# Output projection with prepared weight rows, and a down projection in parts of 3, 4 and 4: one edit to a decoder trunk on one core

## The chip, the cores and the metric

The kernel runs on one core of a Trainium2 chip. The metric is the device time of one launch in microseconds (us); of several executions the median counts. A profile shows one execution, and its span runs from the first to the last instruction. The engines are TensorE (PE in the profile; its weight loads are PEld), VectorE (DVE), ScalarE (ACT), GpSimd (POOL) and SyncE (SP), which here issues nearly all DMAs in one queue. Each engine runs its own instructions in program order.

## The reference, cut to what matters

One decoder layer on 2048 tokens (T) of width 1024 (D), all in float32. Two mixers share one input projection. Each one's output is normalised by its own RMS and gain, the two are put side by side and go through one output projection with a residual; then comes a SwiGLU block of hidden width 2816, and a last norm.

```python
def rmsnorm(x, g):
    return x * rsqrt(mean(x * x, axis=-1) + 1e-6) * g

h = rmsnorm(x, norm_mix)
u_a, z_b, xbc_b, dt_b = split(h @ w_in)
y_a = rmsnorm(s5_mixer(u_a, ...), s5_norm)        # 1024 columns
y_b = rmsnorm(ssd_mixer(z_b, xbc_b, dt_b, ...), ssd_norm)   # 1024 columns
x = x + concatenate([y_a, y_b], axis=-1) @ w_out  # w_out: 2048 x 1024
h = rmsnorm(x, norm_ffn)
x = x + (silu(h @ w_gate) * (h @ w_up)) @ w_down  # w_down: 2816 x 1024
return rmsnorm(x, norm_final)
```

The factor `rsqrt(...)` belongs to a token (a "norm factor" below), the gain `g` to a channel (a "channel factor").

## The kernel before, in words

**Products.** A float32 product is made of three matmuls: each operand is split into a high and a low part, and high x high, high x low and low x high add up in one PSUM bank. A split is a copy on ScalarE (high) and a subtraction on VectorE (low; in the input projections on GpSimd, L69).

**Stages, in order of time.** First the input projections of token half 0 (`project` with tiles `us`, `xs`, `zs`: S5 inputs, convolution channels, gate), beside which VectorE makes the S5 tables (`s5_tables`, about 123 to 241 us); the same for half 1; then the S5 scans, the SSD mixer in quarters and the gated linear unit of S5 (`glu`) to 1213 us. From there on all products are of the Winograd form (L1130): a 2 x 2 block product in seven block products instead of eight, of sums of blocks. One call of `winograd` has seven products `P1` to `P7`; each takes n row blocks x three matmuls of 128 x 512 (L1155), so 84 matmuls with n = 4 and 63 with n = 3. The stationary operands (A11, A12, A22 and the sums S1 to S4) come from tokens, the moving ones (B11 to B22 and the sums T1 to T4) from weights or, in the up part, the other way round. The seven results are added to residual tiles `x`: an "end" is one addition on VectorE out of PSUM (L1161); a "kept" partial sum, on which a later product goes on in the same bank, is copied by ScalarE into a small tile `sg` (L1166), and VectorE adds the copy (L1168).

**Output projection** (`mixed_out`, 1213 to 1585 us). Round r = 0 takes the S5 rows of w_out, r = 1 the SSD rows, each with eight tiles of 256 tokens. For a tile, `normed` (L1194) loads the tokens `st`, makes a diagonal matrix `dg` of their norm factors (L1202), spreads it over all partitions by a matmul with ones (`ps_iv`, L1204), and multiplies each of eight channel blocks by channel factor and norm factor (L1208). `stationary_operands` (L1100) then makes and splits the seven operands of the tile, VectorE doing the sums and low parts (L976). Seven splits of B operands happen once for each round: those of r = 0 ahead of its first tile in `mixed_out`, those of r = 1 within the last tile of r = 0 by `next_rows` (L1067), which loads raw weight blocks, makes the sums T1 to T4 on VectorE between the splits, and hangs each split behind the product that frees its buffer (`after`, L1169). During the last tiles of r = 1, `NextTokens` (L1030) prepares the first operands of the up part and transposes tokens on TensorE (L151). After each tile of r = 1 the norm factors of its two 128-token chunks come out of `norm_stats` (L87): about eight small instructions on VectorE for each chunk.

**Up part** (`ffn_up`): two token halves of 22 calls each, 1585 to 2467 us.

**Down projection** (`ffn_down`, L1328): three rounds over the rows of w_down, each adding to the residual that a DRAM array carries (`x1D`, `x2D`, `x3D`; load at L1350, store at L1356). The rounds have n = 4, 4 and 3 (`down_rows`, L1317), eight tiles of 256 tokens each. The turn from one round to the next is made by `next_rows` again. In the last round a tile also gets its final norm: squares on ScalarE (L1363), the factor on VectorE (`norm_stats`), the multiplication by factor and gain (L1367), and the store of the output (L1368). The `x` tiles come from one tag of four buffers (`t4`), two for each tile of tokens.

**What sets the order.** The program is written stage by stage, but a list scheduler with a simulated time line places the instructions on each engine; `high_priority()` moves a block ahead, and `issue_after(i)` keeps it behind instruction i. A tile waits for its buffer until the last reader of the one before has finished. `take(i, ...)` gives the large slot s*i*.

## Time and profile before

| what | value |
|---|---|
| median of 3 runs | 2949.43 us (2948.5 to 2951.28) |
| the profiled execution | 2948.97 us, its span 2947.2 us |
| mean granted TensorE clock | 0.976 of full speed |
| PE, PEld busy | 95%, 76% of the span |
| DVE, ACT, POOL busy | 71%, 40%, 19% |
| HBM read, written | 263.86 MB, 132.12 MB |

How to read the rows that follow. A group of instructions has line, engine, operation, output <- inputs (names without buffer numbers), partitions x elements and count; then busy us, mean ns of one; then the idle time just ahead of them and what ended most of it. A stretch (`from:to`) has its length and the busy time of PE, PEld, DVE, ACT and POOL (with counts), the granted clock, the mean busy share of the DMA engines, and GB/s; a short form has only PE and PEld. A wait has engine and operation, what it waited for, the sum in us, the count and the longest.

### The profile page before, as it was taken

What the parts mean: (1) busy time and instruction counts of PE and PEld (TensorE: products, weight loads), DVE (VectorE), ACT (ScalarE), POOL (GpSimd) and SP (SyncE); (2) the same over time, 40 slices, a digit from 0 to 9 for tenths busy, and PEclk for the clock granted to TensorE, in tenths of its full rate; (3) what the DMA queues carried; (4) which work ended last, traced back from release to release, by engine and by line L of the source; (5) the groups of instructions that cost most, each with busy time, mean ns of one, the idle gap of its engine ahead of it and who ended that gap; (6) DMA issues with size and microseconds to landing.
All of it is one profiled execution on the core that took longest, in us unless ns stands there. A gap on an engine that the chain in (4) does not pass through costs nothing.

```text
span 2947.2 us, 35852 instructions
## 1 busy us (share of the span) xinstructions
PE 2797.5 (95%) x13020; PEld 2244.4 (76%) x13020; DVE 2087.4 (71%) x3937; ACT 1177.6 (40%) x1853; POOL 550.2 (19%) x462
## 2 busy tenths in 40 slices
PE   7999999998999989899898999998999999999986
PEld 6777877777877867687676888886888887878875
DVE  7398049989768788988789555557555558686786
ACT  4244234556553343433335333334333334243442
POOL 2364111124666767200000000000000000000000
PEclk9999999999999999899999999999999999999998
DMA  7256345543446464644553222223322224555444
GB/s 182 80 158 195 107 133 153 165 131 100 135 145 193 148 185 128 197 168 147 143 169 118 86 86 86 96 80 100 112 86 81 73 78 173 175 179 193 164 142 136
DMA packets 314873, 398.33 MB, mean 135 GB/s; under 512 B 32492, under 2 KB 232280, under 8 KB 314696
## 3 DMA queue, kind: packets, MB, share of 16 engines
q1 hardware_dynamic: 314696, 396.04, 42.6%
q8 instruction: 103, 1.69, 0.2%
q14 instruction: 74, 0.61, 0.1%
HBM read 263.86 MB, written 132.12 MB: 134 GB/s over the span
## 4 chain that ended last, share of the span: by engine, by line
PE 41%; DVE 10%; DMA 6%; issue 1%; ACT 0%; SPq 0%; DVEq 0%; ACTq 0%
PE ps_w L1155 40%; DMA s<-ybD 2%; DVE s L976 2%; DMA out_dram<-x 1%; DVE x L1161 1%; DVE s L1208 1%; DMA s<-actD 1%; DVE s L1014 1%; DVE wS L976 1%; DVE wA L976 1%; DMA x<-x3D 1%; DVE x L1168 1%; DVE x L1367 0%; DMA x<-xaD 0%; DVE sum L1115 0%
## 5 line engine op out<-in xcount | busy, mean ns | idle before, releaser
L1155 PE MATMUL ps_w<-s,wS 128*128 128x512 f32 x3936 | 956.8, 397 | 32.6 <-DVE s L976 14.0
L1155 PEld LDWEIGHTS ps_w<-s,wS 128*128 128x128 f32 x3936 | 746.9, 190 | 207.2 <-DVE s L976 16.1
L1155 PE MATMUL ps_w<-s,wA 128*128 128x512 f32 x2952 | 738.3, 402 | 33.2 <-DVE x L1161 11.9
L1155 PEld LDWEIGHTS ps_w<-s,wA 128*128 128x128 f32 x2952 | 564.6, 192 | 172.1 <-DVE x L1161 11.8
L971 ACT CAST wS<-sum 128x512 fp32r<-128x512 f32 (+1 forms) x336 | 203.6, 611 | 394.5 <-PE ps_w L1155 201.6
L81 PE MATMUL ps_in<-s,whi 128*128 128x512 f32 x896 | 352.9, 395 | 0.0
L83 PE MATMUL ps_in<-s,wlo 128*128 128x512 f32 x896 | 351.4, 394 | 1.3 <-POOL wlo L69 1.3
L82 PE MATMUL ps_in<-s,whi 128*128 128x512 f32 x896 | 352.2, 393 | 0.0
L976 DVE TENSOR_TENSOR wS<-sum,wS 128x512 fp32r<-128x512 f32 (+1 forms) x336 | 226.2, 676 | 137.7 <-ACT wS L971 137.1
L69 POOL TENSOR_TENSOR wlo<-wst,whi 128x1024 fp32r<-128x1024 f32 x72 | 183.9, 2555 | 371.2 <-ACT whi L66 344.8
L971 ACT CAST wA<-s 128x512 fp32r<-128x512 f32 (+1 forms) x252 | 150.4, 610 | 249.1 <-PE ps_w L1155 166.4
L1161 DVE TENSOR_TENSOR gu<-ps_w,gu 128x512 f32<-128x512 f32 x134 | 92.5, 691 | 153.6 <-PE ps_w L1155 150.0
L83 PEld LDWEIGHTS ps_in<-s,wlo 128*128 128x128 f32 x896 | 168.9, 189 | 40.1 <-issue 3.4
L81 PEld LDWEIGHTS ps_in<-s,whi 128*128 128x128 f32 x896 | 168.8, 188 | 38.7 <-issue 3.1
L82 PEld LDWEIGHTS ps_in<-s,whi 128*128 128x128 f32 x896 | 168.9, 188 | 36.5 <-issue 2.3
L832 POOL TENSOR_TENSOR s<-cm,dtas 128x512 fp32r<-128x512 f32 x128 | 165.9, 1321 | 44.3 <-PE ps_seg L833 44.3
L976 DVE TENSOR_TENSOR wA<-s,wA 128x512 fp32r<-128x512 f32 (+1 forms) x252 | 165.2, 673 | 3.4 <-ACT wA L971 3.3
L1161 DVE TENSOR_TENSOR x<-ps_w,x 128x512 f32<-128x512 f32 x160 | 109.1, 688 | 52.4 <-PE ps_w L1155 52.1
L1166 ACT COPY gu<-ps_w 128x512 f32<-128x512 f32 x134 | 78.1, 585 | 142.7 <-PE ps_w L1155 141.0
L1168 DVE TENSOR_TENSOR x<-x,sg 128x512 f32<-128x512 f32 x125 | 85.5, 688 | 66.4 <-ACT sg L1166 37.6
L760 DVE SCALAR_TENSOR_TENSOR acc<-xp,cols,acc 128x1024 f32<-128x1024 f32 x72 | 109.4, 1519 | 26.6 <-ACT acc L758 26.0
L66 ACT CAST whi<-wst 128x1024 fp32r<-128x1024 f32 x72 | 75.4, 1047 | 119.6 <-PE ps_in L82 73.2
(356 smaller groups left out, 3614.5 us busy)
## 6 DMA issues: line engine op xcount, KB each, us to landing
wst<-in_w_in_dram SPq DMA_DIRECT2D x56, 512.0 KB
s<-in_w_gate_dram SPq DMA_DIRECT2D x22, 1024.0 KB
s<-in_w_up_dram SPq DMA_DIRECT2D x22, 1024.0 KB
actD<-gu SPq DMA_DIRECT2D x44, 512.0 KB
s<-actD SPq DMA_DIRECT2D x16, 1024.0 KB
xD<-xo SPq DMA_DIRECT2D x24, 512.0 KB
uD<-ev SPq DMA_DIRECT2D x16, 512.0 KB
zD<-sz SPq DMA_DIRECT2D x32, 256.0 KB
```

The source lines that it names most:

```text
L69: eng.tensor_sub(lo, st, hi.bitcast(F32))
L81: nc.tensor.matmul(ps, wh[:, i, :], rh[:, i, :], start=(i == 0), stop=False)
L82: nc.tensor.matmul(ps, wh[:, i, :], rl[:, i, :], start=False, stop=False)
L83: last = nc.tensor.matmul(ps, wl[:, i, :], rh[:, i, :], start=False, stop=(i == n - 1))
L760: V.scalar_tensor_tensor(acc, tap(i), col(i), acc, op0=MUL, op1=ADD)
L832: G.tensor_mul(r, bc(k.tri.unsqueeze(1), [P, 4, P]), bc(part, [P, 4, P]))
L971: a = k.nc.scalar.copy(op[:, 0], raw)
L976: b = eng.tensor_sub(op[:, 1, part], raw[:, part], op[:, 0, part].bitcast(F32))
L1155: nc.tensor.matmul(ps, a[:, p, i, :], b[:, q, i, :], start=(root == name and i == 0 and p + q == 0), stop=(i == n - 1 and p == 1), skip_gr ...
L1161: V.tensor_add(dst, ps, dst if onto else src)
L1166: nc.scalar.copy(dst, bank[root])
L1168: V.tensor_add(block, block, dst)
```

## The change

Four edits go together.

1. **w_out is prepared early, on GpSimd.** A new function `out_rows` runs 16 times between the pairs of tiles of `xs` and `zs` in half 0: two steps follow each pair. A step loads a row block of w_out (of four row blocks, half the columns), multiplies it by the channel factors (2 instructions), makes the sums T1 to T4 (4 subtractions) and stores all eight blocks to a new DRAM array `woD`. In return the low parts of these input weights (L69) are made on VectorE (`lo_pool=False`).
2. **The output projection reads the prepared blocks and leaves the tokens as they are.** `made_rows` takes the place of `next_rows` for r = 1 and only loads and splits. `tokens` takes the place of `normed`: the load alone, without `dg`, `ps_iv` and L1208. Instead `winograd` gets a `scale`: since a row of a product belongs to a token, the norm factor is applied to ends (one VectorE instruction that multiplies and adds) and to kept results (in the ScalarE copy).
3. **Norm factors elsewhere.** In r = 1 `norm_stats` runs once per tile for two chunks, on GpSimd in tiles 0 to 6, on VectorE in the last. The last four additions of squares in `glu` go from GpSimd to VectorE.
4. **Down projection.** The rounds get n = 3, 4, 4 (`PARTS`). In the last round one of a tile's two `x` tiles comes from three further buffers in a free slot, and the final norm's factors are made for both chunks at once, on GpSimd in tiles 0 to 6.

Its core as a diff:

```diff
@@ norm_stats
-    V = k.nc.vector
+    V = k.nc.gpsimd if pool else k.nc.vector
...
-        V.scalar_tensor_tensor(i, t, 1.5, y, op0=ADD, op1=MUL)
+        if pool:
+            V.tensor_scalar(t, t, 1.5, None, ADD)
+            V.tensor_mul(i, t, y)
+        else:
+            V.scalar_tensor_tensor(i, t, 1.5, y, op0=ADD, op1=MUL)
@@ project_pairs
-            w = split_w(k, k.w_in[:, c0 : c0 + P], lo_pool=True)
+            w = split_w(k, k.w_in[:, c0 : c0 + P], lo_pool=lo_pool)
@@ glu
-                nc.gpsimd.tensor_add(sums[:, b], sums[:, b], sq)
+                (V if half and i == KD - 2 else nc.gpsimd).tensor_add(sums[:, b], sums[:, b], sq)
@@ winograd
+    row = {"P2": 0, "P3": 0, "P7": 1, "P4": 1}
+    row_kept = {"P1": 0, "P6": 0, "P5": 1, "P7": 1}
...
-            V.tensor_add(dst, ps, dst if onto else src)
+            if scale:
+                V.scalar_tensor_tensor(dst, ps, scale[row[name]], dst, op0=MUL, op1=ADD)
+            else:
+                V.tensor_add(dst, ps, dst if onto else src)
...
-            nc.scalar.copy(dst, bank[root])
+            if scale:
+                nc.scalar.activation(dst, bank[root], AF.Identity, scale=scale[row_kept[name]])
+            else:
+                nc.scalar.copy(dst, bank[root])
...
+OPS = ("B11", "B12", "B21", "B22", "T1", "T2", "T3", "T4")
+def out_rows(k, w_out, q, area):
+    nc, G = k.nc, k.nc.gpsimd
+    r, kk, e = q // 8, q // 2 % 4, q % 2
+    t = area[:, q % 2]
+    for i in range(2):
+        b = t[:, 2 * i : 2 * i + 2]
+        row = r * 8 + i * 4 + kk
+        src = w_out[row * P : row * P + P, :].rearrange("p (a n) -> p a n", a=2)
+        nc.sync.dma_start(b, src[:, :, e * 256 : e * 256 + 256])
+        G.tensor_scalar(b, b, k.cols[:, C_S5N + row : C_S5N + row + 1], None, MUL)
+    b11, b12, b21, b22, t1, t2, t3, t4 = (t[:, i] for i in range(8))
+    G.tensor_sub(t1, b12, b11)
+    G.tensor_sub(t2, b22, t1)
+    G.tensor_sub(t3, b22, b12)
+    G.tensor_sub(t4, b21, t2)
+    nc.sync.dma_start(k.woD[r, kk, :, :, e * 256 : e * 256 + 256], t)
+def made_rows(k, old, load):
+    m = Moving(k, 4)
+    x = k.spare
+    t = k.take(x, [P, 2, 4, 512], F32)
+    load(t[:, 0], "B11")
+    load(t[:, 1], "T1")
+    r = {}
+    def p1():
+        m.split("B11", old.at["B11"], t[:, 0])
+        load(t[:, 0], "T3")
+    def p2():
+        k.spare = old.at["B21"]
+        r["y"] = k.take(k.spare, [P, 2, 4, 512], F32)
+        load(r["y"][:, 0], "T2")
+        load(r["y"][:, 1], "B22")
+    def p6():
+        m.split("T1", old.at["T2"], t[:, 1])
+        load(t[:, 1], "B21")
+    def p5():
+        m.split("T2", old.at["T1"], r["y"][:, 0])
+        load(r["y"][:, 0], "T4")
+    def p4():
+        m.split("B21", old.at["T4"], t[:, 1])
+        m.split("T4", x, r["y"][:, 0])
+    return m, {
+        "P1": p1,
+        "P2": p2,
+        "P6": p6,
+        "P5": p5,
+        "P7": lambda: m.split("B22", old.at["T3"], r["y"][:, 1]),
+        "P3": lambda: m.split("T3", old.at["B22"], t[:, 0]),
+        "P4": p4,
+    }
@@ mixed_out
+        return lambda dst, name: nc.sync.dma_start(dst, k.woD[r, :, :, OPS.index(name)].rearrange("k p n -> p k n"))
...
-    def normed(r, c, behind=None):
+    def tokens(r, c):
...
-        dg = sp.tile([P, 2, P], F32, name="dg", tag="sq", bufs=1)
-        inv = k.yinv if r else k.ainv
-        for i in range(2):
-            V.tensor_scalar(dg[:, i], k.ident, inv[:, 2 * c + i : 2 * c + i + 1], None, MUL)
-        ps = (k.px)([P, 256], "ps_iv")
-        nc.tensor.matmul(ps, k.ones, dg.rearrange("p a b -> p (a b)"), start=True, stop=True)
-        col = C_SSDN if r else C_S5N
-        with k.tc.issue_after(behind) if behind else nullcontext():
-            for kk in range(KD):
-                V.scalar_tensor_tensor(st[:, kk], st[:, kk], k.cols[:, col + kk : col + kk + 1], ps, op0=MUL, op1=MUL)
...
+        load(x[:, 0], "B11")
+        load(x[:, 1], "T1")
+        st = tokens(0, 0)
+        load(y[:, 0], "T2")
+        load(y[:, 1], "B22")
+        B.split("B11", 7, x[:, 0])
+        B.split("T1", 8, x[:, 1])
...
+        load(x[:, 0], "T3")
+        load(x[:, 1], "B21")
+        B.split("T2", s[1], y[:, 0])
+        load(y[:, 0], "T4")
+        B.split("B22", s[2], y[:, 1])
+        B.split("T3", s[4], x[:, 0])
+        B.split("B21", s[3], x[:, 1])
+        t4 = B.split("T4", s[0], y[:, 0])
...
-                    nextB, ops = next_rows(k, B, 4, load_of(1))
+                    nextB, ops = made_rows(k, B, load_of(1))
...
-                norm_stats(k, k.ss, k.inv, slice(ch, ch + 1))
+            if r:
+                norm_stats(k, k.ss, k.inv, slice(2 * c, 2 * c + 2), pool=c < 7)
+PARTS = ((3, 0), (4, 6), (4, 14))
@@ down_rows
-        n = (4, 4, 3)[r]
+        n, first = PARTS[r]
@@ ffn_down
-                gf = k.take(k.spare, [P, D], F32)
+                area = k.take(k.spare, [P, 4, D], F32)
+                gf = area[:, 0]
...
-                x.append(sp.tile([P, 2, 512], F32, name="x2", tag="t4", bufs=4))
+                if r == 2 and i:
+                    x.append(area[:, 1 + c % 3].rearrange("p (a n) -> p a n", a=2))
+                else:
+                    x.append(sp.tile([P, 2, 512], F32, name="x2", tag="t4", bufs=4))
...
+            for q in (slice(0, 1), slice(1, 2)) if late else (slice(0, 2),):
+                (V if late else nc.gpsimd).tensor_add(s[:, 0, q], s[:, 0, q], s[:, 1, q])
+                norm_stats(k, s[:, 0], iv, q, pool=not late)
@@ trunk_kernel
+    k.woD = dp.tile([2, 4, P, 8, 512], F32, name="woD")
...
-        project(k, 0, h, xs)
+        todo = list(range(16))
+        area = k.take(3, [P, 2, 8, 256], F32)
+        for _ in project_pairs(k, 0, h, xs, lo_pool=False):
+            for _ in range(2):
+                out_rows(k, ins["w_out"][0], todo.pop(0), area)
...
-            project(k, 0, h, zs)
+            for _ in project_pairs(k, 0, h, zs, lo_pool=False):
+                for q in todo[:2]:
+                    out_rows(k, ins["w_out"][0], q, area)
+                todo = todo[2:]
```

**Where instructions move.** VectorE, second round of the output projection, before; `dg`, `nt` and `inv` belong to the norm factors, `s_10406` is the token buffer, `x_` a residual tile, `wS_` an operand:

```order
L1202 TENSOR_SCALAR dg<-cm,yinv 128x128
L1168 TENSOR_TENSOR x_12090<-x_12090,sg 128x512
L976 TENSOR_TENSOR wS_12232<-sum,wS_12232 128x512
L104 SCALAR_TENSOR_TENSOR inv<-nt,ng 128x1
L100 SCALAR_TENSOR_TENSOR nt<-ng,nv 128x1
L104 SCALAR_TENSOR_TENSOR inv<-nt,inv 128x1
L1208 SCALAR_TENSOR_TENSOR s_10406<-s_10406,cols,ps_iv 128x256 x8
```

The same place on VectorE in the changed kernel (`s_10552` is the token buffer):

```order
L1168 SCALAR_TENSOR_TENSOR x_12060<-ps_w,yinv,x_12060 128x512
L980 TENSOR_TENSOR wA_12190<-s_10552,wA_12190 128x512
L1168 SCALAR_TENSOR_TENSOR x_11907<-ps_w,yinv,x_11907 128x512
L980 TENSOR_TENSOR wS_12050<-sum,wS_12050 128x512
L1168 SCALAR_TENSOR_TENSOR x_11905<-ps_w,yinv,x_11905 128x512
```

The steps for the factors and the multiplication of the tokens are gone from VectorE's queue; the additions carry the factor (`yinv`).

GpSimd, while VectorE makes the S5 tables, before; `BD` belongs to the tables, `xp` and `tail` are the convolution's input and its last columns:

```order
L69 TENSOR_TENSOR wlo<-wst,whi 128x1024
L751 COPY xp<-xp 128x8x3x15
L752 COPY xp<-xp 128x7x3
L754 COPY tail<-xp 128x3
L494 MEMSET BD 128x256
```

The same stretch on GpSimd now (`s_1682` is the row block of w_out):

```order
L757 COPY xp<-tail 128x3
L1201 TENSOR_SCALAR s_1682<-s_1682,cols 128x512
L755 COPY xp<-xp 128x8x3x15
L756 COPY xp<-xp 128x7x3
L758 COPY tail<-xp 128x3
L1203 TENSOR_TENSOR s_1682<-s_1682 128x256
```

The low parts have left the queue, and the scalings and subtractions of the row blocks stand between the convolution's copies.

SyncE in the same stretch, before; `wst` are the next input weights, `m1D`, `qD` and `m2D` the stored S5 tables:

```order
L483 DMA m1D<-M_1258 128x1024
L492 DMA qD<-W 128x8x128
L64 DMA wst<-in_w_in_dram 128x8x128
L512 DMA m2D<-Ks 8x16x128
L512 DMA m2D<-Ks 8x16x112
```

And now:

```order
L487 DMA m1D<-M_1259 128x1024
L496 DMA qD<-W 128x8x128
L1207 DMA woD<-s_1682 1024x1x256 x2
L64 DMA wst<-in_w_in_dram 128x8x128
L516 DMA m2D<-Ks 8x16x128
```

Two stores of finished row blocks (`woD`) stand ahead of the load of the next input weights.

## The prediction

> **What bounds the kernel now.** I read first the page's line of busy times. Then I cut the fused Winograd matmuls (line L1155) into stretches: the two rounds of the output projection, the two halves of the up part, the three rounds of the down part, and the tail. Columns: stretch, its length, PE busy (matmuls), weight loads, granted clock, DMA share, GB/s. The last row is a steady 100 us inside the up part, for all engines.
> ```profile
> PE 2797.5 (95%) x13020; PEld 2244.4 (76%) x13020; DVE 2087.4 (71%) x3937; ACT 1177.6 (40%) x1853; POOL 550.2 (19%) x462
> ...
> 1213.00:1392.00 179.00, 166.92 (x673) 130.93 (x674) 0.94 0.48 163
> 1392.00:1585.00 193.00, 169.31 (x675) 130.03 (x674) 0.96 0.52 153
> 1585.00:2026.00 441.00, 430.34 (x1850) 347.68 (x1849) 0.99 0.26 86
> 2026.00:2467.00 441.00, 431.68 (x1850) 348.65 (x1849) 0.98 0.27 91
> 2467.00:2628.00 161.00, 156.39 (x670) 127.52 (x669) 0.98 0.54 189
> 2628.00:2788.00 160.00, 156.87 (x675) 127.06 (x674) 0.99 0.51 175
> 2788.00:2934.00 146.00, 126.49 (x505) 99.59 (x504) 0.93 0.45 141
> 2934.00:2947.20 13.20, 0.51 (x2) 0.00 (x0) 0.63 0.38 118
> ...
> 1700.00:1800.00 100.00, 100.00 (x437) 81.70 (x436) 54.46 (x81) 34.14 (x60) 0.00 (x0) 1.00 0.29 94
> ```
> TensorE bounds the kernel, and where nothing hinders it a matmul takes 100/437 = 0.2288 us, so a tile of 84 takes 19.2 us. The length of a stretch less its count times 0.2288 is what it spends on anything else: 25.0, 38.5, 17.7, 17.7, 7.7, 5.5 and 30.4 us. The change leaves the up part alone; it can win from 25.0 + 38.5 + 30.4 = 93.9 us. A clock below 1.00 is part of that: (1 - 0.94) x 179 = 10.7 us in the first row, 7.7 and 10.2 in the other two. The stretches with few stalls show 0.98 or 0.99, so I let that part go where the stalls go.

> **Output projection.** VectorE's groups in the second round (1392 to 1585), then two TensorE groups over both rounds, then all engines in the second round and the first two tiles of each round (matmuls alone), then one PE wait of the first round.
> ```profile
> L1208 DVE SCALAR_TENSOR_TENSOR s<-s,cols,ps_iv 128x256 f32<-128x256 f32 x56 | 22.7, 476 | 29.1 <-DMA s<-ybD 29.1
> ...
> L976 DVE TENSOR_TENSOR s<-s,s 128x1024 fp32r<-128x1024 f32 x14 | 16.7, 1221 | 0.0
> ...
> L100 DVE SCALAR_TENSOR_TENSOR nt<-inv,nv 128x1 f32<-128x1 f32 x28 | 6.0, 216 | 0.3
> ...
> L95 DVE TENSOR_SCALAR nv<-ss 128x1 f32<-128x1 f32 x14 | 2.1, 150 | 0.1
> ```
> ```profile
> L1204 PE MATMUL ps_iv<-dg,cm 128*128 128x256 f32 x30 | 9.1, 387 | 0.0
> L151 PE MATMUL ps_t<-cm,s 128*128 128x128 f32 x60 | 8.6, 276 | 1.3 <-DVE s L1027 1.3
> ```
> ```profile
> 1392.00:1585.00 193.00, 175.78 (x747) 139.23 (x746) 157.44 (x366) 77.32 (x130) 0.00 (x0) 0.96 0.52 153
> ...
> 1213.00:1249.00 36.00, 27.38 (x86) 18.96 (x87) 0.81 0.41 131
> 1249.00:1275.00 26.00, 23.02 (x87) 18.08 (x87) 0.87 0.51 172
> 1392.00:1423.00 31.00, 24.62 (x88) 17.86 (x87) 0.89 0.36 97
> 1423.00:1449.00 26.00, 22.23 (x90) 17.28 (x89) 0.93 0.58 147
> ...
> PE ps_ss L903 <- POOL suma L950: 2.0, 1, 2.0
> ```
> For each of seven tiles L1208 costs VectorE 22.7/7 = 3.2 us. The norm factors are six groups (the first and the last shown: 6.0 + 4.2 + 3.0 + 2.2 + 2.1 + 2.1 = 19.6), 2.8 us per tile. VectorE is busy 157.4/8 = 19.7 us per tile, more than TensorE's 19.2, and its queue stood 29.1 us at L1208 until tokens had come, with all that was queued behind. Both leave VectorE, and 13 to 14 us remain. The factors on product rows come into additions that exist already (4 per tile, 0.69 before, 0.75 by the L1367 row below: 0.2 us, hidden).

> In VectorE's rows of the second round (shown with the change) the multiplications between token load and splits have gone, and the small steps with them; what is late next is the token load itself, ahead of the first split.

> First round: the first two tiles lose 36 - 86 x 0.2288 = 16.3 and 6.1 us, the other six 2.6 (mostly L1204). The weight sums leave VectorE there (two round turns of 8 x 1.22 = 9.8 us each), and the last GLU sums come to it (4 x 0.69 = 2.8) in place of the 2.0 us wait. But the seven splits stay, and the three last raw weights are now loaded only when a split has freed a buffer. Of 22.4 I take 13 (bounds 6 and 19), and 2 of the 2.6: **-15**.

> Second round: 10.9 + 5.4 us in the first two tiles, 22.2 later, of which 8.6 (L151) stay and about 4 (half of L1204) go, so 9.6 are stalls. I take 10 of the 16.3, the 4, and 8 of the 9.6: **-22** (12 to 27).

> **Down projection.** Two of VectorE's groups in its last round; then, of the chain that ended last, a store's landing and a load (start, us, what); then the first tile of the last two rounds.
> ```profile
> L1367 DVE SCALAR_TENSOR_TENSOR x<-x,fi,s 128x512 f32<-128x512 f32 x28 | 19.7, 746 | 0.1
> ...
> L1168 DVE TENSOR_TENSOR x<-x,sg 128x512 f32<-128x512 f32 x24 | 16.3, 688 | 27.0 <-DMA x<-x3D 27.0
> ```
> ```profile
> 2918.91 6.50 DMA out_dram<-x
> ...
> 2925.47 3.36 DMA x<-x3D
> ```
> ```profile
> 2628.00:2655.00 27.00, 23.86 (x96) 18.47 (x95) 0.94 0.38 135
> 2788.00:2810.00 22.00, 18.18 (x72) 14.21 (x71) 0.92 0.37 131
> ```
> Here a tile has 63 matmuls, 14.4 us, and four x tiles turn in a loop of factors, store, landing (6.5) and load (3.4); VectorE stood 27.0 us for that load. Three more tiles give the loads a lead of a tile, and parts of 4 make the tile 19.2 us. VectorE then needs 7 splits and 12 additions of 0.69 and four L1367 of 0.70: 15.9. Of 30.4 some 10 are left: the first tile with its turn (5.5 now, 7 with larger weights) and 3 of stalls: **-20** (12 to 25). The factor chain on GpSimd is waited for by L1367, which stands half a tile later in the queue. The first round becomes the short one: its start splits fewer rows (-1), its end makes larger weights beside tiles of 14.4 us (5.0 now, 7.5 then): **+1.5** (-1 to 5). In the last tile the factors stay on VectorE: the tail keeps its 13.2 (+-1).

> **Early GpSimd work.** All engines while VectorE makes the S5 tables; PE's wait there; groups of 120 to 285, of the whole run and (the last two) of 800 to 1200.
> ```profile
> 140.00:241.00 101.00, 94.42 (x540) 75.11 (x539) 98.21 (x100) 37.01 (x56) 58.12 (x51) 0.98 0.53 155
> ...
> PE ps_k L501 <- DVE W L491: 6.6, 4, 2.4
> ...
> L69 POOL TENSOR_TENSOR wlo<-wst,whi 128x1024 fp32r<-128x1024 f32 x12 | 31.1, 2592 | 24.1 <-ACT whi L66 24.1
> ...
> L457 POOL TENSOR_SCALAR cc<-cc 128x1024 f32<-128x1024 f32 x1 | 3.0, 3028 | 0.1
> ...
> L426 POOL TENSOR_SCALAR SI<-run 128x32 f32<-128x32 f32 x6 | 1.7, 304 | 0.5 <-DVE run L376 0.3 <-PE ps_in L82 0.2
> ...
> L836 DVE TENSOR_TENSOR L<-L,Gm 128x512 f32<-128x512 f32 x58 | 65.6, 1147 | 14.9 <-ACT L L835 14.9
> ...
> L854 DVE TENSOR_TENSOR E<-E,ps_yd 128x512 f32<-128x512 f32 x30 | 20.4, 679 | 0.3
> ```
> VectorE is busy 98.2 of 101 us, and TensorE waits 6.6 for it. The change hands it eight low parts of weights in this stretch, 8 x 1.22 = 10 us. The scheduler has allowed for it: 57 more matmuls stand between the first and the last table step on TensorE, 13 us. GpSimd sheds 2.6 us per weight tile and gains 5.6 per row block: two scalings (3.0/2 each) and four subtractions of 256 columns (2.6/4 each). Its queue in the table stretch (shown with the change) now has scalings and subtractions of row blocks between the convolution's copies: these, and VectorE behind them, wait for a scaling that waits for a load. In SyncE's rows there the next weights (wst) stand behind a store (woD) that waits for GpSimd. What covers this: a weight buffer is free 48 matmuls, 11 us, ahead of its next use. And 16 x 1.5 = 25 MB of traffic come on top of a DMA share of 0.53. No trace shows the sum of it; the ends are nothing (all covered) and 25 us (ten pairs late by 2.5). I take **+8**, near the 6.6 that the same queue costs now.

> **Sum.** The profiled run took 2948.97, its span 2947.2 and 1.8 around it: 2948.97 - 15 - 22 - 20 + 1.5 + 8 = 2901.5. The median lies 0.5 above that run: **2902**.

> **Rivals.**
> *A, the engines shut each other out (0.14).* L836 reads two operands from SBUF and takes 1147 ns beside a busy GpSimd; L854 with one from PSUM takes 679. Fifteen factor steps per tile at 0.30 (L426) could hold VectorE 4.5 us: the last round needs 15.9 + 4.5 = 20.4 > 19.2, its gain falls to 5 and the second round's to 14: 2925. Against it: steps this short seldom meet a long one. [...]
> *B, GpSimd sets the pace: slower (0.07).* Two row blocks (11.2 us) and two tiles' copies must fit a pair of 96 x 0.2288 = 22.0 us; beyond that, each of ten pairs of weights waits some 6 us behind its woD store, 60 in place of 8: 2954. For it: the full stretch above. Against: GpSimd is busy 58 of 101 us there and gives up the low parts.
> *C, loads decide the turns (0.11).* The weights that wait for a freed buffer come too late, and both first pairs of tiles stay as they are: +13 +10: 2925.
> *D, all is covered (0.08).* No early loss, and 12 more at the turns: 2882.

> **Numbers.** The forecast has the remaining 0.60. The range of 2880 to 2932 holds its bounds, A, C and D, and leaves out B and the far ends. About 0.2% (5.9 us) is what a measurement of this kernel can tell from no change. Slower is B with little beside it, 0.06; same 0.02; faster 0.92.

> **What would show it.** Right: VectorE no longer stands at tokens for 29 us; tiles of the output projection near 19.2 from the third on; clock 0.98 or more there; no wait for x<-x3D; PE's waits for table steps of 8 to 15. Wrong: an output projection whose second round takes over 180, a down part that still waits for x, or an early part that ends over 25 us later.

## The result and the profile after

The changed kernel takes 2918.32 us (median of 4 runs, 2912.32 to 2921.67), the kernel before 2948.97: a ratio of 0.9892 (95% interval 0.988 to 0.9905; the quotient of these two medians is 0.9896). The forecast was 2902 (2880 to 2932), faster; a gain of 47.5 us was worked out and 30.7 came. One execution of the run r_queue below (4565.9 us at a granted clock of 0.56; without it that run's median is 2916.5) and one of the kernel before, beside the last two runs (12771 us), were disturbed and stay out of the ratios.

The profiled execution took 2912.32 us (span 2910.5) and is the shortest of the four. The rows are the same cut as before, by the fused Winograd matmuls (now line L1161): first the two rounds of the output projection, then the three rounds of the down part. Columns: stretch, its length, PE busy (matmuls), weight loads, granted clock, DMA share, GB/s.

```profile
1225.00:1384.00 159.00, 155.18 (x675) 126.05 (x674) 1.00 0.60 208
1384.00:1567.00 183.00, 164.66 (x671) 128.19 (x670) 0.96 0.58 172
...
2449.00:2569.00 120.00, 115.84 (x505) 94.35 (x505) 1.00 0.67 230
2569.00:2737.00 168.00, 159.52 (x674) 127.99 (x673) 0.98 0.53 184
2737.00:2898.00 161.00, 156.78 (x673) 126.64 (x671) 0.99 0.43 139
```

Set against the rows before, from the first matmul of a stage to the first of the next:

| stretch | before | after | difference | forecast |
|---|---|---|---|---|
| up to the output projection | 1213.1 | 1224.6 | +11.5 | +8 |
| output projection, first round | 178.9 | 158.9 | -20.0 | -15 |
| second round | 192.8 | 183.6 | -9.2 | -22 |
| up part | 881.8 | 881.7 | -0.1 | 0 |
| down part | 467.8 | 449.3 | -18.4 | -18.5 |
| tail | 13.1 | 12.6 | -0.6 | 0 |

The sum is -36.7 us, the difference of the two spans. The first round now runs at full clock with 155 of 159 us of matmuls. The second still stands at 0.96 and loses 183 - 671 x 0.2288 = 29.5 us.

One execution is not the median. The experiments below that leave the early part of the changed kernel as it is (r_queue, r_late, vec, d_443, d_x4) began the output projection at 1230.5, 1228.5, 1227.0, 1231.7 and 1229.5 us: the early part costs 14 to 19 us as a rule, and the profiled execution was lucky there. The second round scatters as well: it took 183.6 us above, 176.4 (d_443), 178.0 (d_x4), 183.8 (e_zs) and 185.1 (e_q) in executions with the same code in that round, and 178.5 in vec, which differs there only in where the norm factors are made.

**Early part.** TensorE's waits from 120 to 330 us, and GpSimd's groups there (before, the only wait was 6.6 us for VectorE's table steps):

```profile
PE ps_in L81 <- ACT xp L751: 6.4, 3, 3.5
PE ps_m L485 <- DVE W L480: 2.6, 2, 1.6
PE ps_in L83 <- DVE wlo L69: 2.6, 1, 2.6
PE ps_in L81 <- ACT whi L66: 1.8, 1, 1.8
```
```profile
L1201 POOL TENSOR_SCALAR s<-s,cols 128x512 f32<-128x512 f32 x24 | 56.2, 2349 | 14.6 <-DMA s<-in_w_out_dram 14.6
L1206 POOL TENSOR_TENSOR s<-s 128x256 f32<-128x256 f32 x12 | 13.7, 1142 | 0.2
```

The largest wait is for `xp`, the convolution's input, into which ScalarE empties a bank. Its three places lie at 220.7, 237.0 and 251.6 us. What ScalarE itself waited for there (215 to 255 us), and all of VectorE's waits from 196 to 255 us:

```profile
ACT xp L751 <- DVE acc L764: 11.8, 3, 4.2
```
```profile
DVE W L493 <- DMA qD<-W: 2.5, 2, 1.9
DVE acc L764 <- ACT acc L762: 0.6, 1, 0.6
```

ScalarE can't write while VectorE has not finished reading the buffer (L764), and VectorE is busy 36.9 of these 40 us. GpSimd's copies are late too: ScalarE stood 11.2 us for one that ended at 200.7 us, behind subtractions of a row block, and at 277 us a copy of 0.49 us stood behind a scaling that had waited 7.68 us for its load. But no wait of TensorE was ended by one of these copies directly, and from 255 to 285 us it had no wait at all; how much of VectorE's lateness began with the copies stays open. The second loss is near 290 us, where the low parts (`wlo`), now in VectorE's queue, are late.

**Second round.** VectorE's groups over it, then its first two and its last four tiles, matmuls alone:

```profile
L1168 DVE SCALAR_TENSOR_TENSOR x<-ps_w,yinv,x 128x512 f32<-128x512 f32 x30 | 22.3, 746 | 11.3 <-PE ps_w L1161 11.3
...
L1119 DVE TENSOR_TENSOR sum<-s 128x512 f32<-128x512 f32 x8 | 5.5, 687 | 22.1 <-DMA s<-ybD 22.1
```
```profile
1384.00:1404.00 20.00, 19.14 (x84) 15.28 (x82) 1.00 0.79 213
1404.00:1432.00 28.00, 22.43 (x84) 17.61 (x83) 0.88 0.55 167
1471.00:1496.00 25.00, 20.68 (x85) 15.51 (x85) 1.00 0.58 168
1496.00:1518.00 22.00, 20.43 (x84) 15.40 (x84) 1.00 0.62 193
1518.00:1542.00 24.00, 20.86 (x82) 16.34 (x83) 0.93 0.44 132
1542.00:1567.00 25.00, 22.33 (x88) 16.68 (x87) 0.93 0.51 168
```

The multiplication of tokens is gone (before: 22.7 us busy, 29.1 idle for tokens), and the additions that carry the factor take 746 ns, as costed. But the queue still stands 22.1 us for tokens, now at the first sum (L1119). Why, the chain of work shows from the fifth to the seventh tile (start, us, what):

```profile
1476.24 0.61 DVE wA L980
...
1476.87 9.12 DMA s<-ybD
...
1486.02 0.63 ACT wA L975
...
1501.41 9.16 DMA s<-ybD
```

The last operand of a tile is made (wA on VectorE), 0.02 us later its token buffer is loaded anew, 9 us later the next tile's operands begin. There is one token buffer from the fifth tile on, because the other half of `stage` holds what `NextTokens` prepares.

### The profile page after: what moved, and what is told of

Its sections match the earlier page's. It is cut to its first block, busy times and chain, and to the rows that moved or that the text cites. A ratio compares the mean times of both kernels' runs of the same rounds, so it can differ in the third digit from the quotient of the medians.

```text
span 2910.5 us, 35767 instructions
## 1 busy us (share of the span) xinstructions
PE 2772.4 (95%) x12988; PEld 2227.6 (77%) x12988; DVE 2017.0 (69%) x3544; ACT 1185.9 (41%) x1853; POOL 660.6 (23%) x737
## 3 DMA queue, kind: packets, MB, share of 16 engines
q8 instruction: 102, 1.67, 0.2%
## 4 chain that ended last, share of the span: by engine, by line
PE 69%; DVE 18%; DMA 6%; issue 2%; ACT 2%; SPq 1%; POOL 0%; DVEq 0%; ACTq 0%; POOLq 0%
PE ps_w L1161 47%; PE ps_in L81 4%; PE ps_in L83 4%; PE ps_in L82 4%; DVE s L980 2%; DMA s<-ybD 2%; DVE acc L764 2%; PE ps_glu L81 1%; PE ps_glu L82 1%; PE ps_glu L83 1%; PE ps_st L819 1%; DVE t L564 1%; DVE s L1018 1%; ACT XG L599 1%; PE ps_seg L837 1%
## 5 line engine op out<-in xcount | busy, mean ns | idle before, releaser
L1161 PE MATMUL ps_w<-s,wS 128*128 128x512 f32 x3936 | 951.8, 396 | 29.5 <-DVE s L980 16.7
L1161 PEld LDWEIGHTS ps_w<-s,wS 128*128 128x128 f32 x3936 | 744.8, 190 | 202.6 <-DVE s L980 18.5
L1161 PE MATMUL ps_w<-s,wA 128*128 128x512 f32 x2952 | 722.0, 395 | 20.9 <-ACT wA L975 6.9
L1161 PEld LDWEIGHTS ps_w<-s,wA 128*128 128x128 f32 x2952 | 554.6, 189 | 153.1 <-ACT s L975 9.8
L82 PE MATMUL ps_in<-s,whi 128*128 128x512 f32 x896 | 353.2, 394 | 0.0
L82 PEld LDWEIGHTS ps_in<-s,whi 128*128 128x128 f32 x896 | 169.4, 189 | 36.5 <-issue 2.4
L69 POOL TENSOR_TENSOR wlo<-wst,whi 128x1024 fp32r<-128x1024 f32 x52 | 133.0, 2558 | 281.6 <-ACT whi L66 254.9
L836 POOL TENSOR_TENSOR s<-cm,dtas 128x512 fp32r<-128x512 f32 x128 | 166.7, 1328 | 42.3 <-PE ps_seg L837 42.3
L66 ACT CAST whi<-wst 128x1024 fp32r<-128x1024 f32 x72 | 75.4, 1047 | 131.9 <-PE ps_in L82 85.3
L1180 DVE TENSOR_TENSOR x<-x,sg 128x512 f32<-128x512 f32 x116 | 79.0, 686 | 68.6 <-ACT sg L1178 30.6
L764 DVE SCALAR_TENSOR_TENSOR acc<-xp,cols,acc 128x1024 f32<-128x1024 f32 x72 | 105.4, 1464 | 20.2 <-ACT acc L762 19.7
```

Of the source, the lines that this page charges most:

```text
L69: eng.tensor_sub(lo, st, hi.bitcast(F32))
L82: nc.tensor.matmul(ps, wh[:, i, :], rl[:, i, :], start=False, stop=False)
L764: V.scalar_tensor_tensor(acc, tap(i), col(i), acc, op0=MUL, op1=ADD)
L836: G.tensor_mul(r, bc(k.tri.unsqueeze(1), [P, 4, P]), bc(part, [P, 4, P]))
L1161: nc.tensor.matmul(ps, a[:, p, i, :], b[:, q, i, :], start=(root == name and i == 0 and p + q == 0), stop=(i == n - 1 and p == 1), skip_gr ...
L1180: V.tensor_add(block, block, dst)
```

## The experiments

Tile times below run from a tile's first matmul to the next tile's. Each timed run stands beside runs of the kernel before on the same chip.

### The low parts alone (e_lo)

```diff
-        project(k, 0, h, xs)
+        for _ in project_pairs(k, 0, h, xs, lo_pool=False):
+            pass
...
-            project(k, 0, h, zs)
+            for _ in project_pairs(k, 0, h, zs, lo_pool=False):
+                pass
```

This is the kernel before with nothing else.

> The kernel before with one thing of the change: the low parts of the input weights of xs and zs in half 0 on VectorE, with no row blocks of w_out on GpSimd. In the trace of the changed kernel the output projection starts 11.5 us later than before (1224.6 against 1213.1), and all of it is lost between 210 and 320 us. Theory V (VectorE is full while it makes the S5 tables, and 8 x 1.22 = 10 us more is what it cannot hold): the output projection starts 8 to 12 us later, the time is 2957 to 2961. Theory G (the convolution's copies on GpSimd stand behind scalings of row blocks that wait for loads): here at most 3 us later, 2946 to 2952, since GpSimd has only the copies left.

Measured: 2941.95 us against 2951.94, ratio 0.9965 (0.995 to 0.9981): faster. The output projection starts at 1205.9, 7.1 us earlier than before. Theory V is refuted, and theory G had the size wrong: what I had down as a burden on VectorE is a gain. VectorE's groups from 120 to 240 us, of before, then of this kernel:

```profile
L491 DVE TENSOR_TENSOR W<-W,tq 128x1152 f32<-128x1152 f32 x8 | 15.4, 1927 | 0.1
L489 DVE TENSOR_TENSOR W<-cc,PW 128x1152 f32<-128x1152 f32 x8 | 14.1, 1760 | 1.3 <-DMA qD<-W 1.3
```
```profile
L69 DVE TENSOR_TENSOR wlo<-wst,whi 128x1024 fp32r<-128x1024 f32 x9 | 11.3, 1252 | 4.7 <-ACT whi L66 4.7
...
L489 DVE TENSOR_TENSOR W<-cc,PW 128x1152 f32<-128x1152 f32 x8 | 10.8, 1354 | 0.0
L491 DVE TENSOR_TENSOR W<-W,tq 128x1152 f32<-128x1152 f32 x8 | 10.8, 1345 | 0.0
```

VectorE got 11.3 us of low parts, and two table groups alone gave back 4.6 + 3.3 us, since GpSimd's 2.6 us subtractions no longer ran beside them; a subtraction that takes GpSimd 2.6 takes VectorE 1.25. That this is the cause shows in single steps of the kernel before (start, us, what):

```profile
196.28 1.35 DVE L491 TENSOR_TENSOR W<-W,tq 128x1152 f32<-128x1152 f32 x1
207.22 3.56 DVE L491 TENSOR_TENSOR W<-W,tq 128x1152 f32<-128x1152 f32 x1
```
```profile
207.18 2.39 POOL L69 TENSOR_TENSOR wlo<-wst,whi 128x1024 fp32r<-128x1024 f32 x1
```

The step that began just after a subtraction of GpSimd ended 1.2 us after it, as if it had stood still until then. Two of the eight steps of L491 were such (3.56 and 3.60 us); the other six took 1.35 to 1.52. Over all eight the mean is 1927 ns, against 1345 in e_lo.

So the row blocks' own price is not the net +11.5, but about 1224.6 - 1205.9 = 18.7 us, and more in the other executions. Part of it is paid on VectorE, whose steps are slow again beside them. From 120 to 240 us seven groups of the changed kernel took 8.8 us longer than they would have at this run's means, an estimate from counts and means; one of them, against 1354 ns for the same step (L489) above:

```profile
L493 DVE TENSOR_TENSOR W<-cc,PW 128x1152 f32<-128x1152 f32 x7 | 11.5, 1641 | 2.9 <-DMA qD<-W 2.9
```

### Row blocks after the convolution (e_zs)

```diff
-        for _ in project_pairs(k, 0, h, xs, lo_pool=False):
-            for _ in range(2):
-                out_rows(k, ins["w_out"][0], todo.pop(0), area)
+        project(k, 0, h, xs)
...
-                for q in todo[:2]:
-                    out_rows(k, ins["w_out"][0], q, area)
-                todo = todo[2:]
+                with tc.issue_after(conv):
+                    for q in todo[:4]:
+                        out_rows(k, ins["w_out"][0], q, area)
+                todo = todo[4:]
```

`conv` is the last copy of the convolution. The low parts of the `xs` weights are on GpSimd again.

> The changed kernel with all 16 row-block steps held back until the convolution of half 0 has made its last copy, four for each pair of the gate's tiles; the low parts of xs are on GpSimd again, those of zs on VectorE. Theory G: the loss between 210 and 320 us goes, up to the last convolution tile the trace is that of before (within 2 us). Sixteen steps of 5.6 us, 90 us, then stand in a stretch of 88 us in which nobody waits for GpSimd, so the time is 7 to 12 us below the changed kernel: 2906 to 2911. Rival S (SyncE's queue sets it): the stores of row blocks stand in SyncE's queue ahead of the weight loads of half 1, and what is won is lost there: within 4 us of the changed kernel, 2914 to 2922, or above it.

Measured: 2985.79 us, ratio 1.0121 (1.0103 to 1.0138) to the kernel before: slower than both. The first half of theory G holds: at every 96th input matmul from the 672nd to the 1344th this run is 1.8 to 2.0 us behind before, so nothing is lost in the stretch. But then TensorE stands 73 us at the turn to half 1. ScalarE's wait there, and the chain that ended it (start, us, what):

```profile
ACT s L144 <- DMA woD<-s: 71.9, 1, 71.9
```
```profile
416.69 4.81 DMA woD<-s
421.52 4.12 DMA s<-in_w_out_dram
...
436.81 4.82 DMA woD<-s
441.64 4.26 DMA s<-in_w_out_dram
...
457.75 7.14 DMA woD<-s
465.11 0.70 ACT s L144
```

Rival S named SyncE's queue for such a loss, and it is not that: the first tokens of half 1 (`s L144`) need the slot that the row blocks occupy until the last store has landed. And a pair of steps alone takes 20.1 us (416.69 to 436.81): store, load and GpSimd's work follow each other, so 16 steps take 160 us, not the 90 that I had from GpSimd's work alone.

### The row blocks' transfers on GpSimd's queue (e_q)

```diff
-        nc.sync.dma_start(b, src[:, :, e * 256 : e * 256 + 256])
+        G.dma_start(b, src[:, :, e * 256 : e * 256 + 256])
...
-    nc.sync.dma_start(k.woD[r, kk, :, :, e * 256 : e * 256 + 256], t)
+    G.dma_start(k.woD[r, kk, :, :, e * 256 : e * 256 + 256], t)
```

> The changed kernel with the loads and stores of the row blocks issued by GpSimd and not by SyncE, and nothing else changed. Rival S: SyncE's queue no longer stands behind GpSimd, and the 11.5 us of the early part fall to 4 or less: 2907 to 2912. Theory G: GpSimd still stands at its loads, now with the issuing added to its work, and the convolution's copies behind it are as late as before or later: 2917 to 2930.

Measured: 2915.58 us, ratio 0.9883 (0.9863 to 0.9903), not to be told from the changed kernel; the output projection starts at 1228.4. Taking the transfers out of SyncE's queue does not make the early part shorter. The time itself lies 1.4 us under what theory G gave; its start of the output projection (15 us late) is G's. GpSimd's waits only changed their name: from 120 to 400 us it stood 36.8 us for loads of row blocks before this edit, and here 1.4 us for loads but 36.6 for the landing of its own stores, ahead of the next load into the same buffer.

### The token loads on GpSimd's queue (r_queue)

```diff
-        nc.sync.dma_start(st, src.rearrange("(k p) t -> p k t", p=P))
+        nc.gpsimd.dma_start(st, src.rearrange("(k p) t -> p k t", p=P))
```

> The changed kernel with the token loads of the output projection issued by GpSimd, which is idle there, and not by SyncE. In the second round SyncE's queue holds, ahead of a token load, loads of residual tiles that wait for a store to land and stores that wait for the last addition. Theory Q (this queue makes the tokens late): the second tile of the second round falls from 28.4 to under 22 us, the last four from 24.4, 22.0, 24.1 and 24.5 by 1 to 2 each, 8 to 12 in all: 2906 to 2911. Theory T (from the fifth tile on there is one token buffer, since the other holds what the up part prepares, and the load can only start when the tile's operands are made): the second tile falls as under Q, the last four stay, 5 to 7 in all: 2911 to 2914. Theory L (the loads are slow themselves, 18 us for 1 MB at 150 GB/s): no change, 2916 to 2921.

Measured: 2917.3 us, ratio 0.9882 (0.986 to 0.9904). The second tile fell from 28.4 to 24.2, the last four were 22.1, 28.3, 26.0 and 21.5 (before this edit 24.4, 22.0, 24.1, 24.5), the round 181.7. ScalarE's wait for tokens in that round, in the changed kernel and here:

```profile
ACT wA L975 <- DMA s<-ybD: 34.5, 5, 12.8
```
```profile
ACT wA L975 <- DMA s<-ybD: 35.3, 5, 10.8
```

The sum of waits is the same. Theory Q falls; T's picture (the second tile gains, the last four don't) is met, but its size for the second tile was 6.4 or more and 4.2 came, and other executions with the token loads on SyncE show 26.1 (vec, d_443, d_x4, e_zs) and 29.7 (e_q) there, so that this tile's part stays open between queue and chance.

### Two token buffers for two tiles longer (r_late)

```diff
-        st = stage[:, c % 2 if r == 0 or c < 4 else 0].rearrange("p (k t) -> p k t", t=256)
+        st = stage[:, c % 2 if r == 0 or c < 6 else 0].rearrange("p (k t) -> p k t", t=256)
...
+            if c == 6 and r:
+                ahead = NextTokens(k, 0, tile)
```

> The changed kernel with the up part's first operands prepared from the seventh tile of the second output round on, not from the fifth, so that tokens have two buffers for two tiles longer. In the changed kernel the fifth to eighth tile took 24.4, 22.0, 24.1 and 24.5 us, and the chain of waits there runs through token loads of 9 to 11 us that start when the tile before has made its last operand. Theory T (the single token buffer): the fifth and sixth tile fall to 19.2 to 20.5, the last two keep one such load each and take all of the transposes (8.6 us): the round falls from 183.6 to 175 to 179, the time to 2908 to 2914. Rival W (the preparation's own loads, sums and transposes take the time): it is squeezed into two tiles, the round stays at 182 to 188, the time at 2916 to 2923.

Measured: 2916.02 us, ratio 0.9878 (0.9857 to 0.9899). Fifth tile to the end of the round, then the first two tiles of the up part, here and in the changed kernel (matmuls alone):

```profile
1471.00:1490.00 19.00, 19.00 (x84) 15.48 (x84) 1.00 0.54 165
1490.00:1511.00 21.00, 21.00 (x93) 17.16 (x92) 1.00 0.52 163
1511.00:1537.00 26.00, 21.93 (x86) 16.41 (x85) 0.93 0.55 169
1537.00:1564.00 27.00, 24.18 (x101) 18.25 (x100) 1.00 0.46 156
1564.00:1620.00 56.00, 47.30 (x176) 35.00 (x175) 0.88 0.23 76
```
```profile
1567.00:1617.00 50.00, 42.87 (x176) 33.18 (x175) 0.93 0.20 64
```

Fifth and sixth tile run at 19.3 and 20.5 us and the round at 175.1, as theory T said. In no other run was the fifth tile under 22 us. Of the 6.5 us won in these two tiles some 3.6 may be due to the 33 transposes that left them (about 0.11 us each in the chain, 17 and 16 of them). The last two tiles, which now hold the whole preparation, took no longer (48.4 against 48.7 us). So the single buffer held the fifth tile, which gained 5.1 us; for the sixth, which gained 1.4, this is not shown. But the up part's first 176 matmuls take 56 us in place of 50, because their operands are now prepared too late, and the median falls by no more than the runs scatter. What is won there is given back at the next turn. A further token buffer beside the one that is left was not tried.

### All norm factors on VectorE (vec)

```diff
-                norm_stats(k, k.ss, k.inv, slice(2 * c, 2 * c + 2), pool=c < 7)
+                norm_stats(k, k.ss, k.inv, slice(2 * c, 2 * c + 2))
...
-                (V if late else nc.gpsimd).tensor_add(s[:, 0, q], s[:, 0, q], s[:, 1, q])
-                norm_stats(k, s[:, 0], iv, q, pool=not late)
+                V.tensor_add(s[:, 0, q], s[:, 0, q], s[:, 1, q])
+                norm_stats(k, s[:, 0], iv, q)
```

> The changed kernel with the norm factors of the second output round and of the last down round on VectorE, still for two chunks at once. Theory T: where the factors are made does not matter in the second round (VectorE is busy 11 to 19 us of tiles of 20 to 28) nor in the last (15.9 + 11 x 0.2 = 18.1 of 19.2): within 3 us of the changed kernel, 2914 to 2922. Rival A (GpSimd's steps hold VectorE up): without GpSimd both rounds are shorter, by 4 us or more together: under 2914. Rival F (the factors were late on VectorE, and their leaving was a gain): 5 to 10 us longer, 2923 to 2928.

Measured: 2914.47 us, ratio 0.9875 (0.9855 to 0.9894). The last down round is 161.2 in both, the second output round 178.5, like that of d_x4 (178.0) and d_443 (176.4) with factors on GpSimd. Where the factors are made does not matter for the time, so neither rival A nor F holds in these stages. VectorE does wait for them in the last round of the changed kernel (10.2 us at the final multiplication, L1440), but this round is no longer for it.

### The down part: parts and tiles apart (d_443, d_x4)

```diff
-PARTS = ((3, 0), (4, 6), (4, 14))
+PARTS = ((4, 0), (4, 8), (3, 16))
```

> The changed kernel with the down part in 4, 4, 3 again, and with its further tiles for x and factors on GpSimd. The prediction's step: VectorE needs 15.9 us for a tile of the last round, which with three row blocks has 14.4 us of matmuls. Then this round takes 8 x 15.9 = 127 and a turn of 5 to 7, 132 to 136, the first two 161 each as before: the down part 454 to 458 in place of 449.3, the time 2922 to 2928. Rival X (the wait for x tiles was all of it, the parts do nothing): the last round takes 115 + 8 = 123, the down part 445: 2912 to 2916.

```diff
-                if r == 2 and i:
+                if False:
```

> The changed kernel with the down part in 3, 4, 4 and factors on GpSimd, but all x tiles of the last round from the four buffers that there were. A buffer's turn is its load (3.4), a tile of matmuls, some 5 us of factors and multiplications, and the store's landing (6.5). With tiles of 14.4 that makes 29.7 for two tiles of 28.8, with tiles of 19.2 it makes 34.5 for 38.4. Theory P (the parts alone would have done it): within 4 us of the changed kernel, 2916 to 2922. Rival X (the further tiles do it): the wait for x comes back, 10 to 20 us: 2928 to 2938.

Measured: d_443 2920.14 us, ratio 0.9891 (0.987 to 0.9912); d_x4 2922.74, ratio 0.9904 (0.988 to 0.9927). The scatter of the early part blurs these times, the down part by itself does not:

| down part, us | four x tiles | seven x tiles |
|---|---|---|
| parts 4, 4, 3 | 467.8 (before) | 456.4 (d_443) |
| parts 3, 4, 4 | 458.7 (d_x4) | 449.3 (changed kernel) |

(Before also has the factors on VectorE; in vec, with both edits, their place made no difference.) The last round of d_443 (all engines) and VectorE's largest wait in it; then VectorE's wait for tiles of `x` in the last round of d_x4 and of the changed kernel:

```profile
2774.00:2908.00 134.00, 121.16 (x505) 96.17 (x504) 102.48 (x178) 61.44 (x144) 28.18 (x105) 0.97 0.47 152
```
```profile
DVE sum L1119 <- DMA s<-actD: 9.0, 2, 6.2
```
```profile
DVE x L1180 <- DMA x<-x3D: 22.1, 6, 4.8
```
```profile
DVE s L1180 <- DMA s<-x3D: 2.0, 1, 2.0
```

In d_443 the last round took 133.6 us where the matmuls alone would make 115. That is the number expected, but not for its reason: VectorE was busy 102 of 134 us and not 127, two of its tiles ran at 14.4 and 14.5 us, and what it waited for most were loads of its input (`actD`). So the step that VectorE needs 15.9 us for a tile is refuted and the hit was luck; what makes this round longer with parts of 3 stays open. In d_x4 the wait for x tiles comes back with 22.1 us, though TensorE loses only 7.7 by it: the turn of a buffer (34.5 estimated against 38.4) was worked out too short, and both theories missed, P from below and X from above. One edit alone brings 9 to 11 us, the two together 18.4.

### The row blocks where engines are free (split_q, split)

Eight steps for the first round stand after the last convolution copy, two for each pair of the gate's tiles; eight for the second round in the first four tiles of the first output round. The low parts of the first tiles of half 1 go to VectorE too.

```diff
+        for _ in project_pairs(k, 0, h, xs, lo_pool=False):
+            pass
+        todo = list(range(8))
...
+            for _ in project_pairs(k, 0, h, zs, lo_pool=False):
+                with tc.issue_after(conv):
+                    for q in todo[:2]:
+                        out_rows(k, ins["w_out"][0], q, area)
+                todo = todo[2:]
...
+            if first:
+                area = k.take(6, [P, 2, 8, 256], F32)
+            if r == 0 and c < 4:
+                for q in range(8 + 2 * c, 10 + 2 * c):
+                    out_rows(k, ins["w_out"][0], q, area)
```

With the transfers issued by GpSimd:

> The changed kernel with the 16 row-block steps taken out of the crowded stretch: eight (for the first output round) after the last convolution copy of half 0, two for each pair of the gate's tiles, and eight (for the second round) in the first four tiles of the first output round; loads and stores of row blocks issued by GpSimd, low parts of xs, zs and of the first tiles of half 1 on VectorE. Theory G (the early loss is the row blocks' time on GpSimd beside convolution and tables; the low parts on VectorE are a gain of 8, as the run with them alone showed): the output projection starts at 1205 to 1212, not at 1225 to 1231; the first round stays at 160 to 164, since it has no stalls and VectorE is busy 14 of 19.2 us: 2895 to 2903. Rival A (GpSimd and VectorE shut each other out): eight steps of 5.6 us take up to 45 us from VectorE in four tiles that leave it 4 x 5 us, and the first round is 10 to 25 longer: 2908 to 2925.

And by SyncE:

> The same with loads and stores of row blocks issued by SyncE. Theory G with a queue that does not matter: as with GpSimd's issues, within 3 us of it. Rival S (SyncE's queue): a pair of steps took 20 us where they stood alone, so SyncE's queue stands behind GpSimd's stores, and weight loads at the turn to half 1 and token loads of the first output round come late behind it: 5 to 20 us longer than with GpSimd's issues.

Measured: split_q 2902.79 us, ratio 0.9849 (0.9827 to 0.9871); split 2899.74, ratio 0.9835 (0.9815 to 0.9854). Both beat the changed kernel (0.988 to 0.9905) clear of its interval. The further low parts on VectorE bring nothing by themselves: from the hundredth input matmul on, split is 0.2 to 2.0 us behind e_lo, which has neither them nor row blocks, and at the start of the output projection 0.8 us (1206.7 against 1205.9). GpSimd's scalings in split from 300 to 400 us, and the two rounds of its output projection:

```profile
L1201 POOL TENSOR_SCALAR s<-s,cols 128x512 f32<-128x512 f32 x12 | 18.7, 1565 | 31.1 <-DMA s<-in_w_out_dram 31.0
```
```profile
1207.00:1369.00 162.00, 157.35 (x670) 127.38 (x669) 0.98 0.81 279
1369.00:1551.00 182.00, 165.68 (x678) 129.73 (x677) 0.96 0.59 176
```

The output projection starts at 1207 (1208 in split_q), 18 us before the changed kernel's, and the first round takes 163 (161) us with GpSimd at work beside it. A scaling takes 1.57 us here; in the changed kernel from 120 to 330 us, with VectorE busy 173 of 210 us, it took 2.35. GpSimd again stands 31 us for loads, but TensorE has no wait that ends in it. Theory G is met within its range, rival A and rival S are not.

## Why the prediction was nearly right, and where its steps failed

- **Early GpSimd work, +8: the sign held, the sum was made of wrong parts.** +11.5 in the profiled execution, 14 to 19 in others, within the 0 to 25. I had "5.6 per row block: two scalings (3.0/2 each) and four subtractions of 256 columns (2.6/4 each)"; in the crowd it was 2 x 2.35 and four of about 1.03 (the mean of four groups, 0.92 to 1.14): 8.8. And "hands it eight low parts ... 10 us" was counted as a load on VectorE; alone that move gains 7 to 10. The convolution's copies behind a scaling that waits for a load were named and are in the trace, but none of TensorE's waits ends at one; what the sum left out is that VectorE's own steps slow down beside GpSimd's (8.8 us from 120 to 240 us). The weights behind `woD` stores in SyncE's queue were named too; without them in that queue nothing was won (e_q). PE's waits for table steps were 4.4 us and not the 8 to 15 given as a sign: the rest of its waits is for the convolution's input and for weights.
- **First round, -15: -20.** The first two tiles gained 17.5 us where 13 were taken (bounds 6 and 19); the second lost nothing any more (19.2). The six later tiles gained 0.4 each. The other runs in which this round is unchanged took 159.6 to 161.1 us, a gain of 17.8 to 19.3.
- **Second round, -22: -9.2, and -7.7 to -16.4 in other executions of the same code.** The sign "over 180" that was to show the forecast wrong came (183.6), and so did a clock below 0.98 (0.96). The failed step is "9.6 are stalls ... 8 of the 9.6". I named the token load as what would be late next and then took its stalls away all the same: from the fifth tile on they are in good part the single token buffer's, which the change leaves as it was (r_late). The last six tiles gained 2.4 us where 12 were forecast.
- **Down part, -18.5: -18.4.** The agreement is luck in part. The last round lost 7.8 us (10 forecast) and the first round's start less than forecast, but the turn to larger weights lost 13.6 (7.5 forecast), and these errors cancel. All engines over the last round but its first tile (PE, PEld, DVE, ACT, POOL):

```profile
2757.00:2898.00 141.00, 139.15 (x605) 112.98 (x603) 101.22 (x161) 60.62 (x130) 28.73 (x105) 1.00 0.44 140
```

  VectorE was busy 101.2 us for 605/84 = 7.2 tiles, 14.1 per tile, less than the 15.9. The 15.9 adds up durations, but additions that follow each other overlapped in the trace: those of 0.68 us start 0.60 apart (in the changed kernel's second output round, at 1389.86, 1390.46 and 1391.06 us).
- **The rest of the distance** is the median's: it lies 6 us above the profiled execution. No trace shows where; in the runs that leave the early part as it is, that part ended 2.4 to 7.1 us later than in the profiled execution.
- **Rivals.** A fits the early part as far as times go (1641 ns for the step L493 against 1354 in e_lo), though that the engines shut each other out is not shown, and it is false where I had put it, in the factor steps: that one of them on GpSimd holds VectorE for its 0.30 us no run shows, and the last down round takes 161.2 us with them on either engine (vec). B's condition was met: two steps of 8.8 and the copies of two tiles (3.1 each) make 23.8 against 22.0, but the loss was 19 in all and not 6 us for every pair. C was right that loads decide in the second round, but loads of tokens, not of weights. D is out.

## What to carry to other kernels

Work that is moved to an idle engine is priced by the stretch where it lands, not by its busy time: by what its neighbours slow down to, by what stands behind it in that engine's queue, and by the buffer it holds; measure the move and what is moved in return apart, since here one was a gain of 7 us and the other a loss of 19. When an engine's work ahead of a wait is removed, look for the buffer whose release starts the load: if that is unchanged, the wait can stay and only its name change, as here from 29.1 us at L1208 to 22.1 at L1119.

## What the runs showed of the hardware that was not expected

GpSimd's scaling of 128 x 512 took 1.57 us in split from 300 to 400 us; in the changed kernel it took 1.67 in that stretch, where VectorE was busy 24.7 of 100 us, and 2.35 where VectorE was busy 173 of 210 us (120 to 330 us). The table steps with two SBUF operands took 1.93 us on the average in the kernel before and 1.35 without GpSimd's subtractions (e_lo), and the difference sits in the two of eight steps that began just behind a subtraction (3.6 us). So both sides took longer. In the first output round GpSimd was busy 45 of 77 us in split, and the round took 162.9 us against 158.9 to 161.2 without it: with VectorE busy 60 of the 77 us, GpSimd's work beside it cost little.

TensorE's clock went down beside a wait of 2.0 us and stayed up beside one of 2.8. Its waits in the fifth tile of the second round of the changed kernel, and in the eighth:

```profile
PE ps_w L1161 <- ACT wA L975: 2.8, 1, 2.8
```
```profile
PE ps_w L1161 <- ACT sg L1176: 2.0, 1, 2.0
```
